# The first loads of a windowed-attention kernel: a quarter of the first q over SyncE, all else issued by GpSimd at once

## The chip, the cores and the metric

One core of a Trainium2 chip. The time is the device time of one execution in microseconds (us); a program on one core has no slower sibling to compare with.

## The reference

Attention inside windows of 64 rows, over 4 x 4096 rows of 1536 columns:

```python
def reference(q, k, v):                 # q, k, v: [4, 4096, 1536] float32
    B, S, D = q.shape
    W = 64
    nw = S // W
    scale = D ** -0.5
    q_w, k_w, v_w = (x.reshape(B, nw, W, D) for x in (q, k, v))      # shortened
    logits = np.einsum('bnwd,bnud->bnwu', q_w, k_w) * scale
    logits = logits - logits.max(axis=-1, keepdims=True)
    attn = np.exp(logits)
    attn = attn / attn.sum(axis=-1, keepdims=True)
    out = np.einsum('bnwu,bnud->bnwd', attn, v_w)
    return out.reshape(B, S, D).astype(np.float32)
```

Inputs are 302 MB, the output 100.7 MB, all float32.

## The kernel before

The rows are worked through in 32 units of 512 rows. A unit has one load each of q, k and v (3.146 MB of HBM each, cast to float16 on the way by a DMA that GpSimd issues) and one store of 3.146 MB. Loads land in two landing buffers for each of q, k and v; GpSimd copies a landed buffer to the working buffer (the hand-over), tells the compute engines, and requests the load two units on. Cuts are marked.

```python
    def hand_over(x, u, dst, m, g):
        gp = nc.gpsimd
        gp.wait_ge(landed[x][u % NL], 16 * ((u + u % NL) // NL))   # its DMA has landed
        gp.wait_ge(m, u)                                           # the unit before is done with dst
        gp.tensor_copy(out=dst..., in_=landing[x][u % NL]...).then_inc(c_l, 1)   # cut
        ...
        gp.sem_inc(g, 1)
        request(x, u + NL)
    ...
        gp = nc.gpsimd
        for u in range(1, N):
            hand_over("q", u, q16, m_q, g_q)
            hand_over("k", u, k16, m_k, g_k)
            gp.wait_ge(m_q, u + 1)
            store(u - 1)
            hand_over("v", u, v16, m_v, g_v)
```

The first unit is different: its q comes as float32, in four pieces issued by SyncE, into the first output buffer `outs[0]`, and GpSimd casts it from there. GpSimd waits for the first piece before it issues anything. That prologue is the "-" side of the diff below.

The softmax here doesn't subtract the row's maximum and nothing guards it: scores larger than these inputs give would overflow.

Of the kernel before, what the change touches and what calls it, by code (L numbers as in the profile page):

```python
# [17 lines left out]
def kernel(  # L18
# [13 lines left out]
    nc = tc.nc  # L32
    PE, DVE, ACT = (getattr(mybir.EngineType, e) for e in ("PE", "DVE", "Activation"))
    B, S, D = q.shape
    DC = D // (2 * P)
    NJ = D // 512
    SLOTS, R, H = 4, 2, 2
# [3 lines left out]
    qf, kf, vf, of = (x.rearrange("b s d -> (b s) d") for x in (q, k, v, out))  # L41

    def sb(name, shape, dtype):
        return ctx.enter_context(nc.sbuf_tensor(name, shape, dtype))
# [6 lines left out]
    def sem(name):  # L51
        sems.append(nc.alloc_semaphore(name))
        return sems[-1]

    q16 = sb("q16", [P, SLOTS, D], FP16)
    k16 = sb("k16", [P, SLOTS, D], FP16)
# [6 lines left out]
    outs = [sb(f"out{i}", [P, SLOTS, D], FP32) for i in range(NO)]  # L63
# [7 lines left out]
    ops = [ps(f"o{j}", [P, 512]) for j in range(NJ)]  # L71
    sp = ps("sp", [P, 4])

    d_r0, d_r1, d_r2, d_r3, d_k0, d_v0 = (
        sem(n) for n in ("d_r0", "d_r1", "d_r2", "d_r3", "d_k0", "d_v0")
    )
    landed = {x: [sem(f"d_{x}{i + 1}") for i in range(NL)] for x in "qkv"}
    d_o = [sem(f"d_o{i}") for i in range(NO)]
    d_l = [sem(f"d_l{i}") for i in range(2)]
    g_q, g_k, g_v = (sem(n) for n in ("g_q", "g_k", "g_v"))  # L80
# [11 lines left out]
    i_d, i_p, c_q, c_l, done = (sem(n) for n in ("i_d", "i_p", "c_q", "c_l", "done"))  # L92
# [4 lines left out]
    def rows(x, row0, n, r):  # L97
        return x[row0 : row0 + P * n].rearrange("(h p r) d -> p h (r d)", p=P, r=r)

    def slots(t, lo, hi, r):  # L100
        return t[:, lo:hi, :].rearrange("p (h r) d -> p h (r d)", r=r)

    def load(name, u, dst, s):
        src = {"q": qf, "k": kf, "v": vf}[name]
        r = R if name == "v" else SLOTS
        nc.gpsimd.dma_start(
            out=slots(dst, 0, SLOTS, r), in_=rows(src, u * UR, SLOTS, r)
        ).then_inc(s, 16)
# [169 lines left out]
    def store(u):  # L278
        nc.gpsimd.dma_start(
            out=rows(of, u * UR, SLOTS, R), in_=slots(outs[u % NO], 0, SLOTS, R)  # L280
        ).then_inc(d_o[u % NO], 16)

    def request(x, u):
        if u < N:
            load(x, u, landing[x][u % NL], landed[x][u % NL])
# [3 lines left out]
    def hand_over(x, u, dst, m, g):  # L289

        gp = nc.gpsimd
        gp.wait_ge(landed[x][u % NL], 16 * ((u + u % NL) // NL))
        gp.wait_ge(m, u)
        gp.tensor_copy(  # L294
            out=dst[:, :, :].bitcast(FP32), in_=landing[x][u % NL][:, :, :].bitcast(FP32)
        ).then_inc(c_l, 1)
        copies[0] += 1
        gp.wait_ge(c_l, copies[0])
        gp.sem_inc(g, 1)
        request(x, u + NL)  # L300

    with tc.tile_critical(no_gpsimd_drain=True):

        raw = rows(qf, 0, SLOTS, SLOTS).rearrange("p h (r d) -> p (h r) d", d=D)
        for lo, hi, c0, c1, s in (
            (0, 1, 0, D // 2, d_r0), (0, 1, D // 2, D, d_r1), (1, 2, 0, D, d_r2), (2, SLOTS, 0, D, d_r3)
        ):
            nc.sync.dma_start(
                out=outs[0][:, lo:hi, c0:c1], in_=raw[:, lo:hi, c0:c1]
            ).then_inc(s, 16)  # L310
        nc.vector.memset(ident[:, :], 0.0).then_inc(i_d, 1)
        nc.gpsimd.wait_ge(i_d, 1)

        nc.gpsimd.wait_ge(d_r0, 16)
        nc.gpsimd.affine_select(
            out=ident[:, :], in_=ident[:, :], compare_op=mybir.AluOpType.not_equal,
            fill=1.0, base=0, pattern=[[-1, P]], channel_multiplier=1,
        ).then_inc(i_p, 1)
        load("k", 0, k16, d_k0)
        load("v", 0, v16, d_v0)  # L320

        for i in range(SLOTS):
            nc.gpsimd.wait_ge((d_r1, d_r2, d_r3, d_r3)[i], 16)
            nc.gpsimd.tensor_copy(out=q16[:, i, :], in_=outs[0][:, i, :]).then_inc(c_q, 1)
            if i == 1:
                request("q", 1)
        for x, u in (("k", 1), ("v", 1), ("q", 2), ("k", 2), ("v", 2)):
            request(x, u)

        nc.vector.memset(ones[:, :], 1.0).then_inc(i_d, 1)  # L330
        nc.vector.memset(zeros[:, :], 0.0).then_inc(i_d, 1)
        for et in ets:
            nc.vector.memset(et[:, :, :, :], 0.0).then_inc(i_d, 1)
        nc.scalar.wait_ge(i_d, 5)
        nc.scalar.activation(zeros[:, 3:4], zeros[:, 0:1], EXP, bias=zeros[:, 0:1], scale=1.0)

        with nc.Fori(0, N, engines=OrderedEngineSet([PE]), head_slot={PE: 0}):
            tensor_unit()
        assert N % NO == 2
        for eng, unit in ((DVE, vector_unit), (ACT, scalar_unit)):  # L340
            with nc.Fori(0, N // NO, engines=OrderedEngineSet([eng]), head_slot={eng: 0}):
                for u in range(NO):
                    unit(u)
            for u in range(N - 2, N):
                unit(u)

        sy = nc.sync
        for j in range(NJ):
            for n in (2, 3):
                sy.sem_inc(f_o[j][n], 1)  # L350
        for a in range(2):
            sy.sem_inc(fr[a], NO)
        sy.wait_ge(i_p, 1)
        sy.wait_ge(i_d, 5)
        sy.wait_ge(c_q, SLOTS)
        sy.sem_inc(g_q, 1)
        sy.sem_inc(g_k, 1)._wait_ge(d_k0, 16)
        sy.sem_inc(g_v, 1)._wait_ge(d_v0, 16)
        for u in range(NO, N):
            sy.wait_ge(d_o[u % NO], 16 * (u // NO))  # L360
            for a in range(2):
                sy.sem_inc(fr[a], 1)
# [10 lines that stand above are left out]
        base, o = (N - 1) * UR, outs[(N - 1) % NO]  # L373
        for h, c in enumerate((1, 3)):
            for a in range(2):
                sy.wait_ge(n_e[a], c)
            sy.dma_start(
                out=rows(of, base + R * P * h, R, R), in_=slots(o, R * h, R * h + R, R)
            ).then_inc(d_l[h], 16)
        gp.drain()  # L380
        gp.sem_inc(done, 1)
        sy.wait_ge(done, 1)
        for i in range(NO):
            last = max(u for u in range(N - 1) if u % NO == i)
            sy.wait_ge(d_o[i], 16 * (last // NO + 1))
        for i in range(2):
            sy.wait_ge(d_l[i], 16)
        lo, hi = min(s.num for s in sems), max(s.num for s in sems)
        assert hi - lo + 1 == len(sems)
        sy.sem_clear(range(lo, hi + 1))  # L390
# [30 lines left out]
```

## Time and profile before

| | before |
|---|---|
| time, three runs | 943.18 us (942.78 to 943.63) |
| span of the profiled run | 941.3 us |
| DMA engines' share | 90% or more in 39 of 40 slices |
| PE, ACT, GpSimd, DVE busy | 70, 36, 36, 30% |
| first transpose on PE | 19.54 us |
| hand-over copy of the second unit's q | 35.33 us |

Every hand-over copy in the fence below waits for its DMA, so the start of a hand-over copy is a clock for the stream of transfers, and the same copy's start in two traces tells how far one stream is ahead of the other. GpSimd's timeline of the kernel before (start, length, instruction, in brackets the idle time and what ended it):

```profile
35.33 2.75 POOL L294 COPY q<-ql 128x3072 f32<-128x3072 f32 x1 [13.20 <-DMA ql<-in_q_dram]
...
79.05 2.74 POOL L294 COPY q<-ql 128x3072 f32<-128x3072 f32 x1 [3.20 <-DMA ql<-in_q_dram]
...
86.33 2.75 POOL L294 COPY k<-kl 128x3072 f32<-128x3072 f32 x1 [3.40 <-DMA kl<-in_k_dram]
...
918.13 2.74 POOL L294 COPY v<-vl 128x3072 f32<-128x3072 f32 x1 [10.55 <-DMA vl<-in_v_dram]
```

### The profile page before, as it was taken

The page shows a single profiled execution, that of the slowest core. Times are in us where ns is not written, and L with a number is a line of the kernel's source. Part 1 is how long each engine was busy: PE and PEld are TensorE (multiplying, and loading weights), DVE is VectorE, ACT ScalarE, POOL GpSimd, SP SyncE. Part 2 cuts the span into 40 slices and gives each one's busy share as a digit, 9 for nine tenths or more (in the row PEclk, how much of TensorE's full clock was granted, in tenths as well). Part 3 has the DMA queues.
Part 4 walks back from the last instruction along what each step waited for, and adds up shares of the span by engine and source line. Part 5 has one row for each costly group of instructions (what it writes and reads, how often), then busy time and mean ns, then how long its engine had stood idle before and what let it go on. Part 6 is the DMA issues. An engine that isn't in the chain of part 4 may idle for free. (4 is left out here: it accounts for less than half of the span.)

```text
span 941.3 us, 11422 instructions
## 1 busy us (share of the span) xinstructions
PE 655.5 (70%) x4096; PEld 395.4 (42%) x3456; DVE 279.8 (30%) x453; ACT 335.9 (36%) x642; POOL 340.4 (36%) x228
## 2 busy tenths in 40 slices
PE   1888676866777768677677686776767768667672
PEld 1555344533455334444244543444433445334440
DVE  0433322333313323133332233322333223332231
ACT  1444433333333333333433324433333323343332
POOL 4344333344333443333423334333343333433221
PEclk9999978889878888888888878978888888898887
DMA  9999999999999999999999999999999999999998
GB/s 247 216 217 281 254 247 281 282 281 263 239 280 283 281 271 232 280 282 281 277 234 273 281 281 282 238 264 282 280 282 248 253 284 279 281 257 245 283 297 366
DMA packets 27084, 253.35 MB, mean 269 GB/s; under 512 B 2112, under 2 KB 2112, under 8 KB 10688
## 3 DMA queue, kind: packets, MB, share of 16 engines
q0 software_dynamic: 26208, 246.95, 100.0%
q1 hardware_dynamic: 864, 6.29, 1.7%
q14 instruction: 10, 0.08, 0.0%
q8 instruction: 2, 0.03, 0.0%
HBM read 301.99 MB, written 100.66 MB: 428 GB/s over the span
## 5 line engine op out<-in xcount | busy, mean ns | idle before, releaser
L157 PE MATMUL lt<-xq,xk 128*128 128x256 f16 x1536 | 215.5, 292 | 0.0
L145 PE MATMUL tp<-ident,k 128*128 128x128 f32 x768 | 149.1, 339 | 84.8 <-PEq L211 74.7
L294 POOL COPY v<-vl 128x3072 f32<-128x3072 f32 x31 | 85.2, 2747 | 296.0 <-DMA vl<-in_v_dram 296.0
L157 PEld LDWEIGHTS lt<-xq,xk 128*128 128x128 f16 x1536 | 159.6, 104 | 33.0
L145 PEld LDWEIGHTS tp<-ident,k 128*128 128x128 f32 x768 | 115.5, 176 | 104.7 <-issue 102.1
L145 PE MATMUL tp<-ident,q 128*128 128x128 f32 x768 | 109.7, 289 | 71.1 <-DVE xq L220 37.0
L220 ACT COPY xk<-tp 128x512 f32<-128x512 f32 x96 | 59.3, 618 | 264.0 <-ACTq L211 264.0
L186 PEld LDWEIGHTS <-et 128*128 128x128 f16 x384 | 34.5, 108 | 283.0 <-issue 277.2
L145 PEld LDWEIGHTS tp<-ident,q 128*128 128x128 f32 x768 | 89.2, 148 | 111.0 <-issue 110.4
L220 DVE COPY xk<-tp 128x512 f32<-128x512 f32 x96 | 66.5, 693 | 229.0 <-DVEq L211 229.0
L294 POOL COPY q<-ql 128x3072 f32<-128x3072 f32 x31 | 85.0, 2742 | 109.9 <-DMA ql<-in_q_dram 109.9
L294 POOL COPY k<-kl 128x3072 f32<-128x3072 f32 x31 | 85.2, 2747 | 107.6 <-DMA kl<-in_k_dram 107.6
L113 PE MATMUL o<-v,et 128*128 128x512 f16 x384 | 113.6, 440 | 0.0
L113 PE MATMUL sp<-ones,et 128*128 128x1 f16 x256 | 25.7, 170 | 116.6 <-PEq L211 114.3
L262 ACT ACTIVATE et<-lt,zeros 32x128 f16<-32x128 f32 x256 | 92.0, 360 | 39.4 <-ACTq L211 36.2
L220 ACT COPY xq<-tp 128x512 f32<-128x512 f32 x96 | 59.8, 623 | 122.1 <-ACTq L211 122.1
L249 DVE TENSOR_SCALAR out<-o,rs 128x512 f32<-128x512 f32 x128 | 91.1, 747 | 33.6 <-DVEq L211 29.6
L273 ACT ACTIVATE out<-tp,rs 128x512 f32<-128x512 f32 x64 | 44.0, 687 | 139.7 <-ACTq L211 112.9
L220 DVE COPY xq<-tp 128x512 f32<-128x512 f32 x96 | 66.3, 690 | 90.0 <-DVEq L211 89.8
L113 PE MATMUL tp<-v,et 128*128 128x512 f16 x256 | 91.9, 446 | 0.0
L239 DVE RECIPROCAL rs<-sp 128x2 f32<-128x2 f32 x64 | 10.7, 168 | 264.8 <-DVEq L211 264.8
L113 PE MATMUL lt<-v,et 128*128 128x512 f16 x128 | 58.3, 456 | 0.0
(21 smaller groups left out, 224.0 us busy)
## 6 DMA issues: line engine op xcount, KB each, us to landing
out_dram<-out POOLq DMA_DIRECT2D x31, 3072.0 KB, 61.8
ql<-in_q_dram POOLq DMA_DIRECT2D x31, 1536.0 KB, 54.9
kl<-in_k_dram POOLq DMA_DIRECT2D x31, 1536.0 KB, 54.9
vl<-in_v_dram POOLq DMA_DIRECT2D x31, 1536.0 KB, 54.9
out_dram<-out SPq DMA_DIRECT2D x2, 1536.0 KB, 9.7
out<-in_q_dram SPq DMA_DIRECT2D x1, 1536.0 KB, 13.9
k<-in_k_dram POOLq DMA_DIRECT2D x1, 1536.0 KB, 13.1
v<-in_v_dram POOLq DMA_DIRECT2D x1, 1536.0 KB, 19.7
```

What stands on the lines that cost most here:

```text
L113: return nc.tensor.add_instruction(mybir.InstMatmult(name=nc.get_next_instruction_name(), engine=PE, ins=[low(rhs), low(w)], outs=[low(o)] ...
L145: ins = nc.tensor.transpose(tps[g % 2][:, r, j, :], pairs[:, c * P : (c + 1) * P], ident[:, :])
L157: ins = nc.tensor.matmul(lts[h][:, r, :, :], lhsT=halves(xk, c)[:, r, h, :, w], rhs=halves(xq, c)[:, :, h, :, w], start=(c == 0 and w == 0 ...
L186: ld = nc.tensor.ldweights(w)
L220: copy(out=dst, in_=tps[g % 2][:, :, :, :]).then_inc(f_c[g % 4], 1)
L239: ve.reciprocal(out=rs[:, n : n + R], in_=sp[:, n : n + R]).then_inc(n_d, 1)
L249: ins = ve.tensor_scalar_mul(scaled(u, n, j), bank(n, j), scalar1=rs[:, n : n + 1])
L262: ins = sc.activation(ets[h][s, :, :, s], lts[h][s, :, :, s], EXP, bias=zeros[s, 0:1], scale=scale)
L273: ins = sc.activation(scaled(u, n, j), bank(n, j), COPY, bias=0.0, scale=rs[:, n : n + 1])
L294: gp.tensor_copy(out=dst[:, :, :].bitcast(FP32), in_=landing[x][u % NL][:, :, :].bitcast(FP32)).then_inc(c_l, 1)
```

## The change

Its intent: start GpSimd's part of the stream at once, behind a small head start over SyncE, rather than after it. SyncE brings only the first of the four rows of each partition; GpSimd brings the other three as a cast load, straight to float16, and then all of k, v and the next two units. One of the four casts on GpSimd remains.

```diff
--- before.py
+++ after.py
@@ -71,9 +71,7 @@
     ops = [ps(f"o{j}", [P, 512]) for j in range(NJ)]
     sp = ps("sp", [P, 4])
 
-    d_r0, d_r1, d_r2, d_r3, d_k0, d_v0 = (
-        sem(n) for n in ("d_r0", "d_r1", "d_r2", "d_r3", "d_k0", "d_v0")
-    )
+    d_r0, d_q0, d_k0, d_v0 = (sem(n) for n in ("d_r0", "d_q0", "d_k0", "d_v0"))
     landed = {x: [sem(f"d_{x}{i + 1}") for i in range(NL)] for x in "qkv"}
     d_o = [sem(f"d_o{i}") for i in range(NO)]
     d_l = [sem(f"d_l{i}") for i in range(2)]
@@ -301,31 +299,24 @@
 
     with tc.tile_critical(no_gpsimd_drain=True):
 
-        raw = rows(qf, 0, SLOTS, SLOTS).rearrange("p h (r d) -> p (h r) d", d=D)
-        for lo, hi, c0, c1, s in (
-            (0, 1, 0, D // 2, d_r0), (0, 1, D // 2, D, d_r1), (1, 2, 0, D, d_r2), (2, SLOTS, 0, D, d_r3)
-        ):
-            nc.sync.dma_start(
-                out=outs[0][:, lo:hi, c0:c1], in_=raw[:, lo:hi, c0:c1]
-            ).then_inc(s, 16)
+        first = rows(qf, 0, SLOTS, SLOTS)
+        nc.sync.dma_start(out=outs[0][:, 0, :], in_=first[:, 0, :D]).then_inc(d_r0, 16)
+        nc.gpsimd.dma_start(
+            out=q16[:, 1:, :].rearrange("p r d -> p (r d)"), in_=first[:, 0, D:]
+        ).then_inc(d_q0, 16)
+        load("k", 0, k16, d_k0)
         nc.vector.memset(ident[:, :], 0.0).then_inc(i_d, 1)
         nc.gpsimd.wait_ge(i_d, 1)
-
-        nc.gpsimd.wait_ge(d_r0, 16)
         nc.gpsimd.affine_select(
             out=ident[:, :], in_=ident[:, :], compare_op=mybir.AluOpType.not_equal,
             fill=1.0, base=0, pattern=[[-1, P]], channel_multiplier=1,
         ).then_inc(i_p, 1)
-        load("k", 0, k16, d_k0)
         load("v", 0, v16, d_v0)
-
-        for i in range(SLOTS):
-            nc.gpsimd.wait_ge((d_r1, d_r2, d_r3, d_r3)[i], 16)
-            nc.gpsimd.tensor_copy(out=q16[:, i, :], in_=outs[0][:, i, :]).then_inc(c_q, 1)
-            if i == 1:
-                request("q", 1)
-        for x, u in (("k", 1), ("v", 1), ("q", 2), ("k", 2), ("v", 2)):
-            request(x, u)
+        for u in (1, 2):
+            for x in "qkv":
+                request(x, u)
+        nc.gpsimd.wait_ge(d_r0, 16)
+        nc.gpsimd.tensor_copy(out=q16[:, 0, :], in_=outs[0][:, 0, :]).then_inc(c_q, 1)
 
         nc.vector.memset(ones[:, :], 1.0).then_inc(i_d, 1)
         nc.vector.memset(zeros[:, :], 0.0).then_inc(i_d, 1)
@@ -352,8 +343,8 @@
             sy.sem_inc(fr[a], NO)
         sy.wait_ge(i_p, 1)
         sy.wait_ge(i_d, 5)
-        sy.wait_ge(c_q, SLOTS)
-        sy.sem_inc(g_q, 1)
+        sy.wait_ge(c_q, 1)
+        sy.sem_inc(g_q, 1)._wait_ge(d_q0, 16)
         sy.sem_inc(g_k, 1)._wait_ge(d_k0, 16)
         sy.sem_inc(g_v, 1)._wait_ge(d_v0, 16)
         for u in range(NO, N):
```

## The prediction

> **What bounds the kernel now.** I read the page first, then the DMA queues by window, the stretches of the first 20 us, the timeline of GpSimd, and the end of the run. Part 2 of the page and its last DMA line:
>
> ```profile
> DMA  9999999999999999999999999999999999999998
> ...
> HBM read 301.99 MB, written 100.66 MB: 428 GB/s over the span
> ```
>
> The digits are the mean busy share of the 16 DMA engines in 40 slices of 23.5 us: 90% or more in all but the last. No compute engine comes near that: PE, the busiest, is at 70% of the span. HBM traffic is 402.65 MB, so the question is only how fast the 16 engines run and when they start. GpSimd's timeline gives the full rate:
>
> ```profile
> 49.91 2.75 POOL L294 COPY v<-vl 128x3072 f32<-128x3072 f32 x1 [2.71 <-DMA vl<-in_v_dram]
> 53.27 0.71 POOL L106 DMA_DIRECT2D vl<-in_v_dram  x1 [0.61 <-POOL v L294]
> 57.20 2.74 POOL L294 COPY q<-ql 128x3072 f32<-128x3072 f32 x1 [3.21 <-DMA ql<-in_q_dram]
> ```
>
> First column the start, second the length; the bracket is the engine's idle time and what ended it. Each hand-over copy waits for its DMA, and two in succession start 7.29 us apart. A load reads 128 x 4 x 1536 float32 = 3.146 MB of HBM, so the engines read 3.146 / 7.29 = 431.5 GB/s. All traffic at that rate takes 402.65 MB / 431.5 GB/s = 933.1 us of the 941.3 us span. Only some 8 us are not pure transfer: about 2 us before the first packet, about 1.6 us after the last (packets end near 939.7), and 4.6 us of weak rate somewhere.
>
> At the end compute isn't the bound either: the last v copy starts at 918.13, the last unit's output is done at 928.65, and the engines still move 424 to 430 GB/s from 920 to 935 us, first the stores queued before. So the time is: start of the stream + work of the stream + what the stream loses.
>
> The only loss the change can touch is at the start. In the timeline, SyncE issues the four pieces of the first q at 0.95 us, and GpSimd waits for the first of them:
>
> ```profile
> 0.95 1.81 SPq L308 DMA_DIRECT2D out<-in_q_dram  x4
> ...
> 7.08 0.28 POOL L315 TENSOR_SCALAR_AFFINE_SELECT ident<-ident 128x128 f32<-128x128 f32 x1 [6.64 <-DMA out<-in_q_dram]
> 7.61 0.68 POOL L106 DMA_DIRECT2D k<-in_k_dram  x1 [0.25 <-issue]
> ...
> 19.54 3.68 PE L145 MATMUL tp<-ident,q 128*128 128x128 f32 x16 [19.54 <-PEq L211]
> ```
>
> The wait of 6.64 us looks large, and PE starts only at 19.54 us. But the stretches show that the DMA engines were at work all the while (last two columns: DMA share, GB/s as landed in the on-chip memory):
>
> ```profile
> 2.00:3.00 1.00, 0.00 (x0) 0.00 (x0) 0.00 (x0) 0.49 (x2) 0.00 (x0) 1.00 1.01 123
> 3.00:4.00 1.00, 0.00 (x0) 0.00 (x0) 0.00 (x0) 0.00 (x0) 0.00 (x0) 1.00 0.92 349
> 4.00:5.00 1.00, 0.00 (x0) 0.00 (x0) 0.00 (x0) 0.00 (x0) 0.00 (x0) 1.00 1.12 412
> ...
> 9.00:10.00 1.00, 0.00 (x0) 0.00 (x0) 0.00 (x0) 0.00 (x0) 1.00 (x2) 1.00 1.02 414
> 10.00:11.00 1.00, 0.00 (x0) 0.00 (x0) 0.00 (x0) 0.00 (x0) 1.00 (x2) 1.00 1.89 283
> 11.00:12.00 1.00, 0.00 (x0) 0.00 (x0) 0.00 (x0) 0.00 (x0) 1.00 (x2) 1.00 0.52 135
> 12.00:13.00 1.00, 0.00 (x0) 0.00 (x0) 0.00 (x0) 0.00 (x0) 0.39 (x1) 1.00 0.97 197
> 13.00:14.00 1.00, 0.00 (x0) 0.00 (x0) 0.00 (x0) 0.00 (x0) 0.00 (x0) 1.00 0.87 184
> ```
>
> The drop from 414 to about 200 is mostly a change of unit: the q pieces land as float32, one byte per byte read; the GpSimd loads land as float16, half a byte per byte read, and their 216 GB/s is 432 of reading. What is really lost is small; it is counted below.
>
> **What the Trainium skill says.** "DMA: Bandwidth & Descriptors", section "Issuing engines are not separate DMA queues": DMAs of all issuing engines run on the same 16 engines and interleave; issuing from several saves only issue time. The trace agrees: the share stays near 1 as the work passes from SyncE's queue to GpSimd's. The same page, "Specifications", puts the fabric ceiling at 435 GB/s; 431.5 here is 99% of it, so there is no headroom. The same page, "SWDGE vs HWDGE vs iDMA", allows a cast in a DMA only from GpSimd: that is why the SyncE pieces land as float32 and need a copy. Its table "Latency and other measured facts" gives a first byte after about 0.6 us from SyncE and 1 us from GpSimd. Here it is longer: SyncE's first packet comes just under 2.0 us (1.05 us after the issue), GpSimd's at about 10.1 us, 2.5 us after the issue began at 7.61. I use the measured ones.
>
> **The change, part by part.**
>
> Bytes: three quarters of the first q land as float16 rather than float32, 1.18 MB less written on chip. HBM reading is unchanged at 3.146 MB, and float32 at 412 to 415 GB/s and cast loads at 216 x 2 = 432 show that the read side sets the pace. Worth: nothing beyond the 4% between those two, 0.1 us on 2.4 MB.
>
> Copies on GpSimd: four casts of about 1.48 us become one. Off the path, since GpSimd then waits 13.20 us for the next q (35.33 us). Worth: 0 at the end. The unit 0 transposes can start once the larger q load has landed, about 11 us instead of 19.54. Also 0 at the end: the next unit's data is paced by the stream, and a unit's work (19.54 to about 41.4, 22 us) fits in the steady cycle of 29.2 us with 7 us to spare.
>
> Losses of the stream up to 20 us, against 431.5 KB of reading per us, with GpSimd's landed bytes doubled by the queue view:
> - 2 to 4 us, first ramp: 123 + 349 = 472 of 863 KB; 391 KB lost, 0.91 us.
> - 4 to 10 us: 2518 of 2589 KB; 0.16 us.
> - 10 to 14 us, hand-over: SyncE 0.12, 0.05, 0.01, 0.00 MB and GpSimd 0.16, 0.09, 0.18, 0.18 MB doubled are 1.40 of 1.73 MB; 0.33 MB lost, 0.76 us.
> - 14 to 20 us: 0.01 + 2 x 1.25 of 2.59 MB; 0.19 us.
> Sum 2.0 us: the most there is to win, apart from the start of the first packet, which stays SyncE's at 2.0 us.
>
> After: GpSimd issues at about 0.95 us instead of 7.61; its first packet is then due at 0.95 + 2.5 = 3.4 us. SyncE's quarter is 0.786 MB; the same ramp brings 0.47 MB by 4 us and the rest by about 4.8 us. So the two queues overlap for some 1.4 us, and the hand-over falls partly inside the first ramp. I take away the 0.76 us and give back half of it (0.38, an estimate: GpSimd's weak second from 11 to 12 us outlasts the overlap), take 0.3 us of the first ramp because a second queue fills it, and half of the 0.16 and 0.19 us (0.17). Sum: 0.76 - 0.38 + 0.30 + 0.17 = 0.85 us, about 0.9.
>
> Order of the queue: the loads come in the same order (q, k, v, then the next units), and each later request still hangs on a landing. So the saving at the start should be carried unchanged to the end: 943.18 - 0.9 = 942.3 us.
>
> **The rivals.**
> 1. *Compute was the bound.* PE's start 8 us earlier would come through, near 935 us. For: the late 19.54. Against: every hand-over waits for a DMA (GpSimd's wait for v alone sums to 296 us), and the 7 us of slack in each unit.
> 2. *Wholly hidden.* The hand-over loss only moves, since GpSimd's queue has to ramp anyway: 943.0 to 943.3. For: the DMA share hardly falls below 0.9. I can't exclude it.
> 3. *All the loss goes.* Both ramps coincide: 2.0 us saved, 941.2. For: GpSimd has 0.95 to 3.4 us to prepare while SyncE feeds the engines. Against: a ramp of some kind remains.
> 4. *It turns slower.* The quarter runs out before GpSimd's packets come, or nine loads and more in the queue stall GpSimd's issuing, so that its one cast and the identity come late. Against: at 21.4 us seven loads are in flight already without a stall of the issues, and the cast is wanted only at 11 us. A hole of 1 us would make it 944.
>
> **Range and chances.** The three runs before span 942.78 to 943.63, 0.85 us. Rivals 2 and 3 give 941.2 to 943.3; with that spread and a little for rival 4, 940.7 to 943.9 us. A change of 2% is 18.9 us, nine times the whole loss at the start: faster 0.01, same 0.98, slower 0.01.
>
> **What would show it.** GpSimd's first load is issued before 1.5 us with its first packet near 3.4; the dip at 10 to 13 us is gone; the first transpose is near 11 us; the hand-over copy of the second q, 35.33 us before, starts near 34.4; the later ones are early by the same amount, still 7.29 us apart; the DMA row remains all nines. I am wrong if those copies move by 4 us or more, if they move early and the end does not follow, or if the load rate departs from 431.5 GB/s.

## More of the kernel before

I call a load "the fourth k" when it belongs to the fourth unit.

The fourth k comes 7.28 us after the fourth q: full rate, no stretch.

## The result, and the profile after

The median is 942.90 us (942.36 to 943.42, 6 runs) against 943.12 us before (6 runs). The ratio of the two is 0.9997 with a 95% interval of 0.9985 to 1.0010; ratios here are the mean time of one kernel's runs over that of the other's of the same rounds, so not quite the ratio of the medians. Predicted were 942.3 us and 940.7 to 943.9.

The page of the changed kernel has the same DMA row and the same HBM traffic:

```profile
DMA  9999999999999999999999999999999999999998
...
HBM read 301.99 MB, written 100.66 MB: 428 GB/s over the span
```

The start did what it was meant to. The timeline after:

```profile
0.95 0.38 SPq L303 DMA_DIRECT2D out<-in_q_dram  x1
...
1.48 0.68 POOL L304 DMA_DIRECT2D q<-in_q_dram  x1 [1.04 <-SPq L300]
...
6.56 0.77 POOL L104 DMA_DIRECT2D vl<-in_v_dram  x1
7.30 1.51 POOL L319 CAST q<-out 128x1536 f16<-128x1536 f32 x1
...
34.47 2.75 POOL L292 COPY q<-ql 128x3072 f32<-128x3072 f32 x1 [25.66 <-DMA ql<-in_q_dram]
```

GpSimd issues from 1.48 us, is through with all nine loads by 7.33, and the hand-over copy of the second q starts at 34.47 us instead of 35.33: the stream is 0.86 us ahead. The stretches of the start after (last columns: DMA share, GB/s as landed):

```profile
2.00:3.00 1.00, 0.00 (x0) 0.00 (x0) 0.00 (x0) 0.49 (x2) 0.93 (x3) 1.00 0.75 160
3.00:4.00 1.00, 0.00 (x0) 0.00 (x0) 0.00 (x0) 0.00 (x0) 1.00 (x3) 1.00 1.10 403
4.00:5.00 1.00, 0.00 (x0) 0.00 (x0) 0.00 (x0) 0.00 (x0) 1.00 (x3) 1.00 1.29 321
5.00:6.00 1.00, 0.00 (x0) 0.00 (x0) 0.00 (x0) 0.00 (x0) 1.00 (x2) 1.00 0.95 194
```

At 4 to 5 us 0.18 MB came over SyncE's queue and 0.12 MB over GpSimd's; counting the latter twice, 0.42 MB were read, full rate but for 3%. The hand-over hole of 0.33 MB at 10 to 14 us is gone, and the first transpose moved from 19.54 to 12.89 us.

But the saving did not reach the end. The same two hand-over copies as before, after the change:

```profile
78.19 2.74 POOL L292 COPY q<-ql 128x3072 f32<-128x3072 f32 x1 [3.21 <-DMA ql<-in_q_dram]
...
86.12 2.75 POOL L292 COPY k<-kl 128x3072 f32<-128x3072 f32 x1 [4.04 <-DMA kl<-in_k_dram]
...
917.38 2.74 POOL L292 COPY v<-vl 128x3072 f32<-128x3072 f32 x1 [10.54 <-DMA vl<-in_v_dram]
```

The fourth q is still 0.86 us early (79.05 - 78.19). The fourth k comes 7.93 us later rather than 7.28, so it is only 0.21 us early. In one load, 0.65 of the 0.86 us is gone. Of the 32 packets of 12,288 bytes that started from 81 to 83 us, 27 took 1.0 to 1.6 us; the median of the loads' packets of that size just before is 0.93. The last v's copy, 918.13 us before, is at 917.38 in this trace, half of that because the trace before had a stretch of its own at 813 us (0.4 us). These traces differ by 0.7 us in span, the medians by 0.2.

### The profile page after: what moved, and what is told of

Same layout as the page of the kernel before. It is cut to its first block, busy times and chain, and to the rows that moved or that the text cites. A ratio compares the mean times of both kernels' runs of the same rounds, so it can differ in the third digit from the quotient of the medians.

```text
span 940.6 us, 11416 instructions
## 1 busy us (share of the span) xinstructions
PE 660.8 (70%) x4096; PEld 399.9 (43%) x3456; DVE 280.0 (30%) x453; ACT 335.8 (36%) x642; POOL 337.3 (36%) x226
## 5 line engine op out<-in xcount | busy, mean ns | idle before, releaser
L143 PE MATMUL tp<-ident,q 128*128 128x128 f32 x768 | 112.6, 294 | 65.4 <-DVE xq L218 34.6
L143 PEld LDWEIGHTS tp<-ident,q 128*128 128x128 f32 x768 | 91.3, 151 | 106.3 <-issue 105.6
## 6 DMA issues: line engine op xcount, KB each, us to landing
q<-in_q_dram POOLq DMA_DIRECT2D x1, 1152.0 KB, 11.1
```

Source lines behind the costliest of these rows:

```text
L143: ins = nc.tensor.transpose(tps[g % 2][:, r, j, :], pairs[:, c * P : (c + 1) * P], ident[:, :])
```

## The experiments

Twelve runs followed, two of them repeats, in four groups, each beside runs of the kernel before on the same chip (the groups were on four different chips). All gave correct results. Of each edit the main lines are shown; further semaphores, waits and the casts' matching lines are cut. "Second q" is the start of its hand-over copy, "stretch" the time from the fourth q's copy to the fourth k's (full rate: 7.28), "last v" the start of the last hand-over copy. In wait_gone and full_at_once the stretch reads short because the fourth q's own copy starts late: GpSimd is still busy with a v.

| kernel | second q | stretch | last v | median us | ratio to before (95%) |
|---|---|---|---|---|---|
| before, first trace | 35.33 | 7.28 | 918.13 | 943.12 | |
| b2: before again | 35.07 | 7.28 | 918.13 | 943.10 | 1.0000 (0.9986 to 1.0014) |
| other_buffer | 35.35 | 7.27 | 917.61 | 942.85 | 1.0000 (0.9985 to 1.0016) |
| wait_gone | 35.32 | 6.96 | 917.82 | 942.96 | 1.0000 (0.9987 to 1.0014) |
| full_at_once | 34.82 | 7.07 | 917.78 | 942.82 | 0.9999 (0.9983 to 1.0016) |
| changed, first trace | 34.47 | 7.93 | 917.38 | 942.90 | 0.9997 (0.9985 to 1.0010) |
| a2: changed again | 33.91 | 8.05 | 918.00 | 943.22 | 1.0004 (0.9990 to 1.0018) |
| spread | 34.12 | 7.93 | 918.19 | 943.23 | 1.0004 (0.9990 to 1.0018) |
| half | 33.73 | 8.21 | 917.98 | 942.90 | 0.9997 (0.9981 to 1.0014) |
| store_late | 34.36 | 7.29 | 918.21 | 943.23 | 1.0001 (0.9986 to 1.0016) |
| pe_late | 40.62 | (late) | 917.91 | 942.91 | 0.9997 (0.9983 to 1.0011) |
| gp_only | 34.23 | 7.97 | 918.78 | 943.82 | 1.0008 (0.9993 to 1.0023) |
| extra_load | 41.34 | 7.98 | 925.58 | 950.26 | 1.0074 (1.0059 to 1.0090) |
| wait_back | 37.46 | 8.02 | 921.91 | 947.77 | 1.0053 (1.0039 to 1.0066) |

The theory after the first result: **the end is set by the stream of transfers alone; the change starts it 0.86 us earlier, and a stall later took it back.** Rivals: the stall is chance (any run has some); the change causes it; compute sets the end after all.

**Both kernels again (b2, a2).** No edit.

> The kernel before once more, unchanged, timed against itself: how far apart two equal kernels come out, and whether the stall of 0.4 us that its first trace shows at 813 us (the hand-over copy of the 28th k came 7.67 us after the one ahead of it, not 7.27) is at the same place. Theory (random stalls of the whole stream): it is elsewhere or absent; the ratio is 1.000 with an interval of about 0.001. Rival (a fixed property of the kernel): a step again at 813 us. Both: the copy of the second q starts at 35.33 +- 0.1 us.

> The changed kernel once more, unchanged. In its first trace the hand-over copies were 0.86 us early up to 79 us, then a stall of 0.65 us at 81 us took most of it. Theory (the saving at the start is carried to the end, and stalls hit any run): the copy of the second q starts at 34.47 +- 0.1, the stall is not at 81 us again, and the median is 0.5 to 0.9 us under that of before. Rival (the change itself causes the stall, by a store or a request meeting the stream earlier): again a step of 0.6 us at 81 us and a saving of 0.2 to 0.3 us at most.

Both in a second trace, before and then changed:

```profile
78.79 2.75 POOL L294 COPY q<-ql 128x3072 f32<-128x3072 f32 x1 [3.19 <-DMA ql<-in_q_dram]
...
86.07 2.76 POOL L294 COPY k<-kl 128x3072 f32<-128x3072 f32 x1 [3.39 <-DMA kl<-in_k_dram]
```

```profile
33.91 2.75 POOL L292 COPY q<-ql 128x3072 f32<-128x3072 f32 x1 [25.11 <-DMA ql<-in_q_dram]
...
77.63 2.74 POOL L292 COPY q<-ql 128x3072 f32<-128x3072 f32 x1 [3.21 <-DMA ql<-in_q_dram]
...
85.68 2.75 POOL L292 COPY k<-kl 128x3072 f32<-128x3072 f32 x1 [4.15 <-DMA kl<-in_k_dram]
```

The stall at 813 us in the first trace before isn't in b2 (its place isn't random, as is told below). The one in the fourth k is there again with the change: 8.05 us in a2, 7.28 in b2. My theory that any run has such a stall, and the saving of 0.5 to 0.9 us that it promised, fell; a2 saves nothing, though its second q is 1.16 us ahead of b2's (35.07 - 33.91). The lead is 0.39 us after the fourth k (86.07 - 85.68), and the last v is 0.13 us early. Both second q missed what I expected within 0.1 us: equal kernels differ there by 0.26 us (35.33, 35.07) and 0.56 us (34.47, 33.91), so a few tenths between single traces show nothing.

**The wait put back (wait_back).**

```diff
+        nc.gpsimd.wait_ge(d_r0, 16)
         nc.gpsimd.dma_start(
             out=q16[:, 1:, :].rearrange("p r d -> p (r d)"), in_=first[:, 0, D:]
```

> The changed kernel with GpSimd's wait for the SyncE quarter put back ahead of its first load: the quarter without the early issue. Theory (the stream's start sets the time): the quarter's bytes are through by about 5 us, GpSimd issues at about 5 to 6 and its packets come 2.5 us later, so the stream has a hole of about 3 us: the copy of the second q at 37 to 38.5 us instead of 34.47, and the time 2.5 to 4 us longer than the changed kernel's (about 945.5 to 946.5). Rival (what comes in the first 10 us is hidden): the time stays within 0.5 us of it.

```profile
5.00:6.00 1.00, 0.00 (x0) 0.00 (x0) 0.00 (x0) 0.00 (x0) 0.00 (x0) 1.00 0.07 25
6.00:7.00 1.00, 0.00 (x0) 0.00 (x0) 0.00 (x0) 0.00 (x0) 0.06 (x1) 1.00 0.06 16
7.00:8.00 1.00, 0.00 (x0) 0.00 (x0) 0.00 (x0) 0.00 (x0) 1.00 (x2) 1.00 0.00 0
```

```profile
37.46 2.75 POOL L292 COPY q<-ql 128x3072 f32<-128x3072 f32 x1 [23.19 <-DMA ql<-in_q_dram]
```

This is what a real hole looks like: three us with hardly a packet, because the quarter is through before GpSimd issues at 6.94 us. The second q is 3.0 to 3.6 us later than in the two traces of the changed kernel, and the time 4.6 us longer than a2's of the same rounds. The hole reaches the end: what is lost at the start is not hidden. I had expected 2.5 to 4. The distance to a2's copies was 3.55 us at the second q (37.46 - 33.91), 4.4 at the ninth k and 3.9 at the last v; small stretches on both sides, nearly all just ahead of a store (see store_late), make it wander.

**The wait gone, the whole q still in float32 (wait_gone).** Without the wait for SyncE's first piece and with k and v issued at once; the four pieces and four casts stay.

```diff
-        nc.gpsimd.wait_ge(d_r0, 16)
+        load("k", 0, k16, d_k0)                 # ahead of ident's memset
         ...
+            if i == 0:
+                nc.gpsimd.wait_ge(d_r0, 16)     # ahead of the first cast only
```

> The kernel before with the wait gone and the first k and v issued at once, but the whole first q still in float32 over SyncE: the early issue without the quarter. Theory (the early issue, not the smaller float32 piece, is what starts the stream better): the copy of the second q near 34.5 +- 0.4 us and the end as in the changed kernel, though q lands later since it shares the engines with k (first transpose at 18 us or after). Rival (the quarter matters): the copy of the second q stays near 35.3.

```profile
24.85 2.88 POOL L325 CAST q<-out 128x1536 f16<-128x1536 f32 x2 [5.69 <-DMA out<-in_q_dram]
28.13 1.94 PE L145 MATMUL tp<-ident,q 128*128 128x128 f32 x8 [28.13 <-PEq L211]
...
35.32 2.75 POOL L294 COPY q<-ql 128x3072 f32<-128x3072 f32 x1 [4.61 <-DMA ql<-in_q_dram]
```

The whole q, sharing the engines with k, is in late: the first transpose is at 28.13 us. The theory fell, and the rival held: the second q is at 35.32, not 34.5. The trace has the reason. A transfer of GpSimd ends with sixteen 4-byte packets, one per DMA engine; the Trainium skill, "DMA: Bandwidth & Descriptors", section "Why a DMA increments its semaphore by 16 and not by 1", says that the engines finish independently and only all sixteen mean that the data is there, and the traces agree (2016 such packets for 126 transfers). The sixteen ends of the first v are spread from 25.18 to 27.70 us before, mean 26.22, and from 24.82 to 27.68 in wait_gone, mean 25.51 (counted from SyncE's first packet, taken to be at 1.98 us in each). The trace doesn't name the engines, so "average" and "slowest engine" here mean the mean and the last of such sixteen ends. The average engine gained 0.7 us, the slowest nothing, and a landing counts by the slowest. After the change they lie from 24.66 to 26.85, mean 25.24: there the slowest gained too. Between stalls the engines keep these distances, since each does its share of a load in 7.28 to 7.31 us: the 2.5 us from first to last end before are still 2.5 us at the fourth k. Over the whole run they drift to 2.3 to 3.3 us in every trace (before from 2.52 to 2.94 at the last v, a2 from 1.67 to 3.10, wait_back from 0.65 to 2.64), so a lead that the slowest engine owes to a narrower start need not last. By the slowest engine the early issue alone wins nothing here; by the average one it wins 0.7 us, of the 1.0 us that the change wins.

**PE held back (pe_late).**

```diff
         sy.wait_ge(c_q, 1)
+        sy.wait_ge(landed["q"][1], 16)
         sy.sem_inc(g_q, 1)._wait_ge(d_q0, 16)
```

> The changed kernel with the first transpose held until the second q has landed (34 us instead of 12.9). Theory (compute has slack, the stream alone sets the end): the first copy of the second q starts some 7 us later because it waits for the transposes, by the fifth unit the hand-over copies are where the changed kernel's are, within 0.5 us, and the time is within 0.5 us of the changed kernel's. Rival (PE's start sets the end): 10 to 21 us longer. The stall ahead of the first store stays at about 81 us, if compute has no part in it.

```profile
35.13 3.69 PE L143 MATMUL tp<-ident,q 128*128 128x128 f32 x16 [35.13 <-PEq L209]
```

The first transpose starts at 35.13 us, 22 us after the changed kernel's, and the time is 942.91 us. At the fifth unit, where I expected 0.5 us, its hand-over copies are 0.9 us behind a2's (0.3 behind the first trace's), by the ninth within 0.8 of a2's, the last v within 0.1. So the 6.65 us by which the change starts PE earlier are worth nothing that these times show, and the rival "compute sets the end" is out. The stretch is there as well (7.91 us for the slowest engine, by the completion packets; the copies themselves are late here), so compute has no visible part in the stall.

**One load more (extra_load).** The first q once more, as float32 into `outs[2]`, not yet in use; the permits to write outputs are given after it has landed.

```diff
         load("v", 0, v16, d_v0)
+        nc.gpsimd.dma_start(out=slots(outs[2], 0, SLOTS, SLOTS), in_=first).then_inc(d_x, 16)
```

> The changed kernel with one more transfer of 3.146 MB (the first q as float32, into an output buffer not yet used) between the first v and the second q. Theory (pure stream): everything after is later by 7.3 us, and so is the time: about 950.4. Rival (the first tens of us are hidden behind compute): under 2 us. The stall of 0.65 us that the three traces with the SyncE quarter show in the load just ahead of the first store: if the first store brings it, it comes at about 88 us, in the same load (the fourth k); if it is tied to the time it stays at 81 us, in the load before that; if it is tied to the count of GpSimd's transfers, likewise in the load before.

The second q is 7.43 us later than a2's, the last v 7.6, and the time 7.3 us longer than before's median of the same rounds (7.0 longer than a2's): 3.146 MB at the stream's rate, undiminished 900 us later. The stall:

```profile
85.08 2.74 POOL L292 COPY q<-ql 128x3072 f32<-128x3072 f32 x1 [3.25 <-DMA ql<-in_q_dram]
...
93.06 2.75 POOL L292 COPY k<-kl 128x3072 f32<-128x3072 f32 x1 [4.09 <-DMA kl<-in_k_dram]
```

It moved with the work, 7.4 us later, and is still in the fourth k. It isn't tied to the time, nor to the count of transfers: the fourth k is GpSimd's twelfth here, the eleventh in the changed kernel.

**The first store one step later (store_late).**

```diff
-            store(u - 1)
+            if u != 1:
+                store(u - 1)
             hand_over("v", u, v16, m_v, g_v)
+            if u == 1:
+                store(0)
```

> The changed kernel with only its first store issued one step later, after the hand-over of the second v: it then follows the fourth v in the queue, not the fourth k. Theory (the stall belongs to the first store): the stretched load is the fourth v (its copy some 7.9 us after that of k rather than 7.3), near 88 us, and the fourth k comes in step, 7.3 us after q. Rival (tied to time or to the count of transfers): the fourth k still comes 7.9 us after q. Both: the time within 0.5 us of the changed kernel's.

```profile
78.08 2.74 POOL L292 COPY q<-ql 128x3072 f32<-128x3072 f32 x1 [3.22 <-DMA ql<-in_q_dram]
...
85.37 2.75 POOL L292 COPY k<-kl 128x3072 f32<-128x3072 f32 x1 [3.40 <-DMA kl<-in_k_dram]
...
93.50 2.74 POOL L292 COPY v<-vl 128x3072 f32<-128x3072 f32 x1 [3.55 <-DMA vl<-in_v_dram]
```

The fourth k comes in step (7.29 us), and the fourth v, now the last load ahead of the first store, takes 8.13 us. So the stall belongs to the load just ahead of the first store, where the stream first changes from reading to writing; why it is there isn't shown. Later stores have smaller ones. Between 100 and 894 us the fourteen traces have 40 transfers whose slowest engine took more than 7.34 us (up to 7.88), and 38 of them are the k load just ahead of a store, though only one transfer in four is such a load; the one at 813 us is among them. By the average engine these take at most 7.40 us, while the load ahead of the first store takes 7.57 to 7.78 in the changed kernel and its relatives.

**All of q by GpSimd (gp_only).** SyncE's quarter and the last cast are gone; GpSimd's load brings all four rows.

> The changed kernel with the whole first q by GpSimd as a cast load, nothing by SyncE. Theory (SyncE's quarter only fills the time until GpSimd's first packets come): the first packets come near 4.2 us instead of 2.0, so the stream starts about 2 us later less the share of the ramp that both have: copy of the second q 1 to 2 us later than the changed kernel's 34.2, time 944 to 945. Rival (the quarter is worth nothing): the same time as the changed kernel's within 0.3 us.

```profile
2.00:3.00 1.00, 0.00 (x0) 0.00 (x0) 0.00 (x0) 0.50 (x2) 0.93 (x3) 1.00 1.03 119
3.00:4.00 1.00, 0.00 (x0) 0.00 (x0) 0.00 (x0) 0.00 (x0) 1.00 (x3) 1.00 0.81 98
4.00:5.00 1.00, 0.00 (x0) 0.00 (x0) 0.00 (x0) 0.00 (x0) 1.00 (x3) 1.00 0.72 147
```

```profile
34.23 2.74 POOL L292 COPY q<-ql 128x3072 f32<-128x3072 f32 x1 [26.89 <-DMA ql<-in_q_dram]
```

(All of it lands as float16: twice that was read.) I expected the second q 1 to 2 us later than 34.2; it is at 34.23, within the range of the changed kernel's two traces. GpSimd's first packets come at 2.9 us here, 1.4 us after the issue at 1.48, not 2.5 or more after it. In wait_back, where the engines were empty too, they come 1.4 us after the issue; in the kernel before 2.4 and in the changed kernel 2.9 us after it, beside SyncE's packets. The 2.5 us that I took for GpSimd's own delay were partly a wait behind SyncE's work. The time, 943.82, is 0.9 us over before's of the same rounds and 0.6 over a2's; of the 0.78 us by which the last v is later than a2's, 0.3 are there at the second q and 0.5 at the ninth unit. The interval includes 1, so the times don't decide. The traces say that the quarter is worth something at the start: the average of the first v's sixteen ends is 25.97 us here against 25.22 and 25.17 in the two traces of the changed kernel. The second q doesn't show it because the ends lie closer here (1.14 us from first to last against 2.19 and 1.67).

**Why is the first store dear in one family only?** Every kernel with the whole q over SyncE has the slowest engine's load ahead of the first store at 7.28 us (full_at_once 7.37), and every kernel with half, a quarter or none has it at 7.66 to 8.19. By the average engine the contrast is softer: 7.28 to 7.42 in the five traces with the whole q, where b2, wait_gone and full_at_once show a stall of 0.1 us that all but spares the slowest engine, and 7.57 to 7.78 in the nine others. Three guesses were tried. The first: the first store reads `outs[0]`, which the whole float32 q has touched and the quarter hardly. other_buffer is the kernel before with its q in `outs[2]`; spread is the changed kernel with the quarter laid over all four slots of `outs[0]`.

```diff
-                out=outs[0][:, lo:hi, c0:c1], in_=raw[:, lo:hi, c0:c1]
+                out=outs[2][:, lo:hi, c0:c1], in_=raw[:, lo:hi, c0:c1]
```

```diff
-        nc.sync.dma_start(out=outs[0][:, 0, :], in_=first[:, 0, :D]).then_inc(d_r0, 16)
+        nc.sync.dma_start(
+            out=outs[0][:, :, : D // 4], in_=first[:, 0, :D].rearrange("p (r d) -> p r d", r=4)
+        ).then_inc(d_r0, 16)
```

> The kernel before with its first q landing as float32 in the third output buffer instead of the first; nothing else differs. In all traces with the whole float32 q in the first output buffer, the slowest engine's load ahead of the first store takes its usual 7.28 us; in all seven with only a quarter of it there or none, 7.88 to 8.14. Theory A (the first store stalls when the transfers haven't touched its buffer before): here the stall appears, 7.9 us for the fourth k's copy after q's, and the time is up to 0.6 us longer than before. Theory B (the larger traffic through SyncE's queue is what spares the stall): no stall, 7.28.

> The changed kernel with SyncE's quarter of q laid over all four slots of the first output buffer (384 of 1536 columns each) instead of filling one slot; same bytes, in rows of 1536 bytes. Theory A (an untouched buffer makes the first store stall): the stall goes or shrinks, the fourth k's copy comes 7.3 us after q's instead of 7.9, and the saving at the start reaches the end: 942.2 to 942.6. Theory B (the amount of SyncE traffic): still 7.9, and 943.0 to 943.3.

```profile
79.08 2.74 POOL L294 COPY q<-ql 128x3072 f32<-128x3072 f32 x1 [3.20 <-DMA ql<-in_q_dram]
...
86.35 2.75 POOL L294 COPY k<-kl 128x3072 f32<-128x3072 f32 x1 [3.40 <-DMA kl<-in_k_dram]
```

other_buffer, in the fence, has no stall (7.27); spread still has it (7.93). Both against the guess: which buffer was touched doesn't matter. The second and third guess, the amount over SyncE and the issue of all loads at once, went into half (two rows of q each way) and full_at_once (all four by SyncE, but all eight loads of GpSimd issued ahead of the casts).

```diff
-        nc.sync.dma_start(out=outs[0][:, 0, :], in_=first[:, 0, :D]).then_inc(d_r0, 16)
+        nc.sync.dma_start(
+            out=outs[0][:, 0:2, :].rearrange("p r d -> p (r d)"), in_=first[:, 0, : 2 * D]
+        ).then_inc(d_r0, 16)
```

```diff
         load("v", 0, v16, d_v0)
+        for u in (1, 2):
+            for x in "qkv":
+                request(x, u)                   # in wait_gone: after the casts
```

> The whole first q as float32 over SyncE, as before, but all eight other first loads issued by GpSimd at once, with the casts after them. So far no kernel with the whole q over SyncE has a stretched last landing ahead of the first store (7.28 us), and all with a quarter or none have (7.66 to 8.14). Theory B (the amount over SyncE, or with it the way the engines are spread over the work, spares it): 7.28 here too. Theory C (issuing all loads at once brings the stall): 7.6 or more, copies of q to k 7.9 us. The time in either case within 0.6 us of before; the second q's copy at about 35.3, as in the kernel with the wait gone, since the slowest engine is set by SyncE's pieces.

> The changed kernel with half of the first q over SyncE and half by GpSimd, all issued at once. Start: the second q's copy at 33.9 to 34.5, as with the quarter, since the stream is fed from 2 us on either way. Theory B by amount: the stretch ahead of the first store falls between, 7.3 to 7.6. Theory C (issue at once) or the count of GpSimd's transfers (one more than before): as with the quarter, 7.66 to 8.14. The time within 0.5 us of the changed kernel's.

full_at_once has hardly any stretch (7.37 us for the slowest engine), so issuing at once doesn't bring it. Its second q is at 34.82 us, not at 35.3 as I expected: with all loads issued at once the whole q over SyncE, too, starts 0.25 to 0.5 us earlier than in the two traces before. half, whose second q at 33.73 us is a little earlier than I expected, has the longest of all (8.21 us by the copies), so it doesn't fall with the amount either. Nor does the distance from first to last end ahead of the stall decide: pe_late has 2.47 us and the stretch, full_at_once 2.23 and hardly any. What separates the families is left open: the whole q over SyncE against any part of it by GpSimd, or, not told apart from that, ten transfers of GpSimd ahead of the first store against eleven or twelve.

No version beat both kernels by more than the spread of equal runs. All but the two that delay or lengthen the stream on purpose lie between 942.8 and 943.8 us.

## Why the prediction was right or wrong

The time fell in the range, and the class was right. The range, 3.2 us wide, holds the kernel before itself, so this says little for the mechanism: the 0.9 us at the end, its real claim, were not found.

- **The bound** (the stream of transfers alone): right. One load more costs 7.3 us of the time, PE 22 us later costs nothing, a hole of some 3 us costs 4.6. (The float32 seconds from 4 to 10 us, read as 412 to 415 GB/s, also hold 390 and 473; their mean is 420, and the reading stands.)
- **The sum of 0.85 us at the start**: 0.86 us in the first trace (35.33 - 34.47), 1.16 in the second pair. By bytes read from 2 to 20 us, counted as the prediction does, the loss fell from 2.10 to 1.17 us, and from 1.87 (b2) to 1.07 (a2). So the size was right, but the hit to a hundredth is luck, for the terms were off and partly cancelled: the hand-over's loss went wholly (0.72 us, in b2 0.41, to none), not by half, and the first ramp gave 0.19 and 0.06 us, not 0.30. Inside the sum, GpSimd's first issue was mis-placed: 1.48 us, not 0.95, and its first packets come at about 4.4 us, not 3.4 (in the kernel before they came at 10.03 us, 2.4 after the issue, a little sooner than I read). First transpose: 12.89 us, not about 11, since the larger q load needs 11.1 us from its issue.
- **"So the saving at the start should be carried unchanged to the end"**: the step that failed. It took every later load to need 7.29 us whatever came before. In the changed kernel and its seven relatives the last load ahead of the first store needs 0.4 to 0.9 us more by its slowest engine, and in the kernel before and its three relatives at most 0.1. That takes back 0.65 and 0.77 us in the two traces of the changed kernel; the small stretches ahead of later stores, different in each trace, blur the rest. The average engine keeps more: its lead is 0.99 and 0.80 us at the first v, 0.43 and 0.62 after the fourth k, 0.64 and 0.51 at the last v. But a landing waits for the slowest. Of the predicted 0.9 us, the medians show 0.2 in one comparison and -0.3 in the other, both inside the spread of equal kernels. No run took the stall out of the changed kernel, so that the time would have fallen without it is argued from the traces, not shown.
- **The rivals.** Number 1 (compute) is out. Number 2 came nearest to the time, about no gain, for the wrong reason: GpSimd's ramp doesn't cost it back, the load ahead of the first store does. Number 3 (all 2.0 us) is out: 0.8 to 0.9 went. Number 4's stalled issues didn't come; nine loads were issued in 5.9 us.
- **The trace checks** that I named hit at the start (dip gone, second q near 34.4, the DMA row), and the one named as a failure came true: the copies moved early and the end did not follow.

## What to carry to other kernels

Where one stream of transfers sets the end, look for microseconds in which the DMA engines move less than full rate, not for late compute: the 6.65 us by which PE starts earlier here were worth nothing, a hole of some three cost 4.6. A landing counts by its slowest DMA engine, so judge a change of the first loads by the spread of the engines as well as by the mean. And follow a saving through the whole trace, load by load, before counting it: here, by the slowest engine, 0.65 of 0.86 us was gone after 86 of 941 us.

## What the Trainium skill lacked or had wrong

- "DMA: Bandwidth & Descriptors", section "Latency and other measured facts": first bytes after about 0.6 us from SyncE and 1 us from GpSimd. Here 1.0 us from SyncE's issue; from GpSimd's 1.4 us on empty engines (gp_only, wait_back) and 2.4 to 2.9 us beside SyncE's packets (before and changed).
- The same page has the sixteen separate completions, but not how far apart they are: 0.65 to 2.86 us at the first v, kept from load to load (before 2.52 there, 2.50 at the fourth k) until a stall changes it, and 2.3 to 3.3 us in all fourteen traces at the last v.
- No page has the stall in the load just ahead of a stream's first store: 7.66 to 8.19 us by the slowest engine for a load that otherwise needs 7.28, or at most 7.37, depending on how the first q is loaded; nor the smaller ones ahead of later stores (38 of the 40 slow transfers). Their cause is open.
